# Order of the first U blocks, the bias rows, and the split of two Wq blocks in a one-core decoder layer

## The chip, the cores and the metric

The kernel runs as one program on one core of a Trainium2 chip. The metric is the device time of one execution in microseconds (us). The time shown is the median of three executions; one further execution was recorded with a profile, and all rows below are from that one. Times in the rows count from the first instruction of the profiled span.

## The reference

One decoder layer over 512 tokens of width 1024, in float32 (cut to what matters here):

```python
a = rmsnorm(h, attn_norm)
proj = a @ w_in                       # q, k, v of both head groups
# differential attention, 4 heads, two maps each, T5 relative bias on both maps
bias = rel_bias[t5_bucket(max(dist, 0))]            # (query, key) -> head
logits = q @ k * scale + bias;  softmax;  attn = probs[0] - lam * probs[1]
# retention, 4 heads; then h += concat(A, B) @ w_out
m = rmsnorm(h, ffn_norm)
scores = (m @ w_query) . sub_keys     # 8 heads x 2 x 128 keys, top 16 of each
expert, gates = the 16 best of the 16 x 16 sums per head, softmax
h += sum over selected e of gate_e * gelu(m . u[e]) * v[e]   # 16384 experts
h += sigmoid(rmsnorm(h) @ Wg + bg) * (p @ Wp)
out = rmsnorm(h, final_norm)
```

## The kernel before, in words

Products of float32 operands are made from two parts of each operand, a rounded high part (`wh`, `xh`) and the rest (`wl`, `xl`), with three products each (`product3`, matmul line 85). Each weight block of 128 x 1024 (512 KB) is loaded by SyncE (SP), its high part is copied by ScalarE (ACT) and its low part is made by a subtraction on VectorE (DVE). In `prepare` there is a second way for the low part: ACT writes the negated high part (line 758), and a DMA on GpSimd's (POOL's) queue adds the raw block to it in place (line 759).

**First stage (attention input).** Token products for one group of values, then the projection blocks in the order of the list `blocks`. `project_tile` multiplies one block and cuts the next one (`ahead`, ACT line 179 and DVE line 185). After the first projection tile come the token scales `rr`/`rT` (lines 132 and 291) and then the bias rows. The T5 bias of a head is a function of the distance alone, so one row of 640 values holds it. `relw` repeats the bias table of each head 128 times, and a product with the one-hot table `bucket` (in two pieces, 512 and 128 columns) gives the row on all 128 partitions; ACT copies the two pieces to `bias_s` (line 341) and POOL's queue stores it in DRAM as `bias_d[h]` (line 342). This is done for four heads in a row. The product tile `pb` has two buffers, which it shares with `rr`. `table(h)` (line 378) later reads `bias_d[h]` back from the same POOL queue with a row step of 639, which gives the Toeplitz table `toep` that the scores of the head add (line 388). POOL also makes copies of half of each q block (line 302) between these DMAs.

**Wq stage.** Sixteen blocks of the expert query matrix, called units ("q", c). Units 0 and 1 are loaded and split while the output projection still runs, with the low part on DVE. Units 2 to 15 use the way over POOL's accumulating DMA. In each step c of the loop at line 965 the kernel issues loads, prepares unit c+2, multiplies unit c, copies the result on ACT (line 981), multiplies the result of step c-1 with its sub-keys (`score`, line 952) and ranks the scores of step c-2 on DVE.

**U stage.** The expert matrix U has 128 blocks. 384 of the tokens meet all experts with a dense product and gate weights that are zero outside the selection; the other 128 tokens fetch their selected rows with indirect DMAs (`gather`, `sparse_step`). The loop at line 1185 multiplies block n, and lets VectorE build the gate weights beside it from a generator (`steps`). The work is placed by hand-written clocks in microseconds (`clock["pe"]`, `["dve"]`, `["dma"]`): a generator step is drawn while the DVE clock is behind the PE clock, and a gathered row or a write of gate weights is placed when the DMA clock lets it. Blocks 0 to 23 (`KEEP`) stay on chip in `kept`; `finish` puts the Gelu of their products there (line 793), and the part of the tokens whose gate weights are already known is multiplied with them by `weigh` (line 799). When the gate weights of 8 tokens come, `tail` multiplies the kept blocks that are done (line 1133, DVE) and copies the weights for those that are not (line 1130, ACT). Blocks from 24 on go out to DRAM: Gelu into `av` (line 809) and a store of 192 KB on SP's queue (`spill`, line 817), one iteration later. After 96 iterations a second loop goes through the V blocks and the rest of U (line 781), and the gate and the final norm end the program.

Of the kernel before, what the change touches and what calls it, by code (L numbers as in the profile page):

```python
# [23 lines left out]
F32 = mybir.dt.float32  # L24
# [11 lines left out]
P = 128  # L36
# [18 lines left out]
def block_kernel(ctx: ExitStack, tc, t):  # L55
# [89 lines left out]
    with pool("wa", 2, side="right") as wa, pool("sm", 2, side="right") as sm, \  # L145
# [67 lines left out]
        with pool("proj", side="right") as pj, pool("att", 2, side="right") as at:  # L213
# [69 lines left out]
                    nc.scalar.activation(val[which, b], ps[b], AF.Copy, scale=ra[:, b:b + 1])  # L283

            first_q = project_tile()
            relw = at.tile([33, 4, P], F32, name="relw", tag="rp")
            nc.vector.tensor_copy(relw, relx[:, :, None].to_broadcast([33, 4, P]))
            rr = psM.tile([P, S], F32, name="rr", tag="misc")
            token_rows(at.tile([P, 4, P], F32, name="dg", tag="rx", bufs=3), rr, ra)
            rT = pj.tile([P, S], F32, name="rT")  # L290
# [42 lines left out]
                dqk[a, m, z] = yield from (stack_q, stack_k)[z](m, x)  # L333


            for h in range(4):
                bias_s = at.tile([P, 640], F32, name="bias_s", tag="pr", bufs=3)
                for x, c0, c1 in bucket:
                    pb = psM.tile([P, 512], F32, name="pb", tag="misc")
                    nc.tensor.matmul(pb[:, :c1 - c0], relw[:, h], x, start=True, stop=True)  # L340
                    nc.scalar.activation(bias_s[:, c0:c1], pb[:, :c1 - c0], AF.Copy)
                nc.gpsimd.dma_start(bias_d[h], bias_s)

            for m, z in ((0, 1), (1, 0), (1, 1)):
                ps = project_tile()
# [389 lines left out]
        def prepare(u, low):  # L735
            kind, i = u
            w = raw.pop(u)
            if kind == "g":
                for d in range(2):
                    c = slice(d * S, (d + 1) * S)  # L740
                    scaled_split(fin["gh"][i][d], fin["gl"][:, i, c], w[:, c], gains[:, G_PLE, i:i + 1])
                return
            wh = wt.tile([P, D], F32R, name="wh", tag="wh")
            wl = wt.tile([P, D], F32R, name="wl", tag="wl")
            nc.scalar.activation(wh, w, AF.Copy)  # L745
            parts[u] = wh, wl
            if kind == "v":
                gv, av = inputs.pop(u)
                if gv is not None:
                    av3 = av.rearrange("p (z t) -> p z t", t=RUN)  # L750
                    nc.vector.tensor_tensor(av3, gv, av3, op=OP.mult)
                ah = vp[0].tile([P, ND], F32R, name="ah", tag="ah", bufs=2)
                al = vp[0].tile([P, ND], F32R, name="al", tag="al", bufs=2)
                nc.scalar.activation(ah, av, AF.Copy)  # L754
                parts[u] += ah, al
            if low is nc.gpsimd:

                nc.scalar.activation(wl, w, AF.Copy, scale=-1.0)
                nc.gpsimd.dma_start(wl.bitcast(F32), w, accum_op=OP.add)
            else:  # L760
                low.tensor_tensor(wl, w, wh.bitcast(F32), op=OP.subtract)  # L761
            if kind == "v":
                nc.vector.tensor_tensor(al, av, ah.bitcast(F32), op=OP.subtract)  # L763

        def products(u):
            kind, i = u
            if kind in "uq":
                n = ND if kind == "u" else S
                wh, wl = (x.rearrange("p (k e) -> p k e", k=KC) for x in parts.pop(u))
                ps = mm.tile([P, S], F32, name="ps", tag="mm")  # L770
                project(ps[:, :n], (wh, wl), mx, slice(0, n))
                made[u] = ps
            elif kind == "v":
                vh, vl, wh, wl = parts.pop(u)
                first, last = count[0] == 0, count[0] == P - 1
                count[0] += 1
                for b in range(NT):
                    c = slice(b * P, (b + 1) * P)
                    for a, bb, f, l in ((wh, vh, first, False), (wh, vl, False, False), (wl, vh, False, last)):
                        for d in range(2):  # L780
                            nc.tensor.matmul(acc[b][d], a[:, c], bb[:, d * S:(d + 1) * S], start=f, stop=l)  # L781
# [140 lines left out]
    with pool("pk") as pk, pool("psG", 2, space=PSUM) as psG, pool("psT", space=PSUM) as psT:  # L922
# [3 lines left out]
        def top16(lists):  # L926
# [8 lines left out]
            for v, ix, src, tmp in lists:  # L935
                nc.vector.max_index(ix[:, 8:16], v[:, 8:16], tmp)

        iof = pk.tile([P, P], F32, name="iof", tag="tmp", bufs=2)
        nc.sync.dma_start(iof, t["iota"])
        io2 = pk.tile([P, P, 2], BF16, name="io2")  # L940
# [1 line left out]
        nc.sync.dma_start(prf[:, :3 * TOPK], t["pairs"])  # L942
        pairs = pk.tile([P, 3, TOPK, TOPK], BF16, name="pairs")
        with pool("qs", 2) as qs:
            units = [("q", c) for c in range(16)] + [("u", n) for n in range(RAW - 1)]
            loaded, prepared = 2, 2
            sks, qt, scores = {}, {}, {}

            def score(c):
                sc = psT.tile([P, 4, P], F32, name="sc", tag="sc")  # L950
                for b in range(4):
                    nc.tensor.matmul(sc[:, b], qt[c][:, b * P:(b + 1) * P], sks[c], start=b == 0, stop=b == 3,  # L952
                                     skip_group_check=True)
                scores[c] = qs.tile([P, 4, P], F32, name="scs", tag="scs", bufs=3)
                nc.scalar.activation(scores[c], sc, AF.Copy)

            def rank(c):
                ic = qs.tile([P, 4, TOPK], U32, name="ic", tag="ic")
                for b in (0, 2):
                    top16([(vals[:, z, c], ic[:, z], scores[c][:, z],  # L960
                            pk.tile([P, P], F32, name="tmp", tag="tmp", bufs=2)) for z in (b, b + 1)])
                nc.vector.tensor_copy(idx[:, :, c], ic)

            for c in range(16):
                while loaded < min(len(units), c + RAW):
                    load(units[loaded])
                    loaded += 1
                while len(sks) < min(16, c + RAW):
                    k = len(sks)
                    sks[k] = qs.tile([P, P], F32, name="sk", tag="sk", bufs=RAW + 1)  # L970
                    nc.sync.dma_start(sks[k], t["sk_t"][k])
                while prepared < min(len(units), c + 3):
                    prepare(units[prepared], nc.gpsimd if units[prepared][0] == "q" else nc.vector)
                    prepared += 1
                if c == 0:
                    nc.vector.tensor_copy(io2, iof[:, :, None].to_broadcast([P, P, 2]))
                    nc.vector.tensor_copy(pairs.rearrange("p z a k -> p (z a) k"),
                                          prf[:, :3 * TOPK, None].to_broadcast([P, 3 * TOPK, TOPK]))
                products(("q", c))
                qt[c] = qs.tile([P, S], F32, name="q", tag="q")  # L980
                nc.scalar.activation(qt[c], made.pop(("q", c)), AF.Copy)
                if c:
                    score(c - 1)
                if c > 1:
                    rank(c - 2)
            score(15)
            rank(14)
            rank(15)
# [195 lines left out]
        n = 0  # L1184
        while busy or later or after or n % QUAD:
            unit[0] = n
            load(("u", n + RAW - 1))
            prepare(("u", n + 2), nc.vector)
            clock["dve"] += 1.25
            for f in after:  # L1190
                clock["dve"] += f()
            after.clear()
            gather()
            spill(0)
            finish(("u", n - 1) if n else None, False)
            clock["pe"] += 4.1
            clock["dma"] = max(clock["dma"], clock["pe"] - BACK) + LOAD + (PART if n > KEEP else 0.0)
            free = [x for x in later if not (writes and writes[0][2] <= x[3] - 2) and n >= x[4]][:2]
            later[:] = [x for x in later if x not in free]
            products(("u", n))  # L1200
            for c, f, a, g, _ in free:
                f(*a)
                clock["pe"] += c
            if soon:
                nc.scalar.activation(*soon.pop(0), AF.Copy)

            for g in {x[3] for x in later if x[1].__name__ == "tail"} | {x[3] for x in free if x[1].__name__ == "tail"}:
                made_at[g] = n
            while (writes and n >= made_at[writes[0][2]] + 2 and clock["dma"] + LOAD <= clock["pe"] + SLACK):
                f, q, g = writes.pop(0)  # L1210
                f(*q)
                clock["dma"] += 1.1 * LOAD
            while clock["dve"] < clock["pe"]:
                c = next(steps, None)
                if c is None:
                    busy = False
                if c is None or c == WAIT:
                    clock["dve"] = max(clock["dve"], clock["pe"] - 5.0)
                    break
                clock["dve"] += SLOW * c  # L1220
            n += 1
# [286 lines left out]
```

## Time and profile before

| | |
|---|---|
| time, median of 3 | 1568.82 us (1565.44 to 1569.31) |
| the profiled execution's own time | 1566.29 us |
| its span | 1564.5 us |
| TensorE (PE) busy | 1525.8 us, 98% |
| VectorE (DVE) busy | 1220.9 us, 78% |
| ScalarE (ACT) busy | 680.2 us, 43% |
| GpSimd (POOL) busy | 384.2 us, 25% |
| mean granted clock of TensorE | 0.991 |

Busy shares are averages over stages with different limits. A busy PE may still run at the lower granted clock, or issue small products.

### The profile page before, as it was taken

The page shows a single profiled execution, that of the slowest core. Times are in us where ns is not written, and L with a number is a line of the kernel's source. Part 1 is how long each engine was busy: PE and PEld are TensorE (multiplying, and loading weights), DVE is VectorE, ACT ScalarE, POOL GpSimd, SP SyncE. Part 2 cuts the span into 40 slices and gives each one's busy share as a digit, 9 for nine tenths or more (in the row PEclk, how much of TensorE's full clock was granted, in tenths as well). Part 3 has the DMA queues.
Part 4 walks back from the last instruction along what each step waited for, and adds up shares of the span by engine and source line. Part 5 has one row for each costly group of instructions (what it writes and reads, how often), then busy time and mean ns, then how long its engine had stood idle before and what let it go on. Part 6 is the DMA issues. An engine that isn't in the chain of part 4 may idle for free.

```text
span 1564.5 us, 22940 instructions
## 1 busy us (share of the span) xinstructions
PE 1525.8 (98%) x8209; PEld 1346.2 (86%) x8209; DVE 1220.9 (78%) x2523; ACT 680.2 (43%) x1077; POOL 384.2 (25%) x311
## 2 busy tenths in 40 slices
PE   8999999899999999999999999999999999999996
PEld 6687888688989999999999889898989898888885
DVE  3577665478998998898995889989888875797755
ACT  5455554444644454344443333333333333353444
POOL 1200000110012203211323556554434210522000
PEclk9899999999999999999999999999999999999999
DMA  6322335775358987987999999999999988899601
GB/s 236 101 81 68 115 101 202 192 177 146 123 174 273 290 277 263 317 289 244 311 324 344 375 340 375 332 383 390 369 341 380 348 326 319 310 404 349 244 23 41
DMA packets 163474, 402.72 MB, mean 257 GB/s; under 512 B 14527, under 2 KB 77258, under 8 KB 163232
## 3 DMA queue, kind: packets, MB, share of 16 engines
q1 hardware_dynamic: 123248, 256.06, 46.3%
q0 software_dynamic: 40112, 145.20, 27.5%
q8 instruction: 64, 1.05, 0.3%
q14 instruction: 50, 0.41, 0.1%
HBM read 350.61 MB, written 42.21 MB: 251 GB/s over the span
## 4 chain that ended last, share of the span: by engine, by line
PE 88%; DVE 5%; DMA 3%; ACT 2%; issue 1%; SPq 0%; POOL 0%; ACTq 0%; DVEq 0%; POOLq 0%
PE ps L85 42%; PE acc L781 33%; PE S L85 3%; PE S L322 1%; PE ps L517 1%; PE pg L1118 1%; PE pg L1120 1%; PE wo L85 1%; DVE wl L761 1%; PE sc L952 1%; PE po L457 1%; DMA wraw<-in_w_val_dram 1%; PE po L638 1%; DMA row<-in_peer_v_dram,e_sp 1%; DMA row<-in_peer_u_dram,e_sp 1%
## 5 line engine op out<-in xcount | busy, mean ns | idle before, releaser
L85 PE MATMUL ps<-xh,wh 128*128 128x384 f32 (+1 forms) x1312 | 464.6, 354 | 3.6 <-ACT av L809 2.7
L85 PE MATMUL ps<-xh,wl 128*128 128x384 f32 (+1 forms) x1312 | 458.1, 349 | 8.8 <-DMA wl<-wraw 4.5
L85 PE MATMUL ps<-xl,wh 128*128 128x384 f32 (+1 forms) x1320 | 458.1, 347 | 0.0
L745 ACT ACTIVATE wh<-wraw 128x1024 fp32r<-128x1024 f32 x272 | 286.8, 1054 | 196.1 <-PE ps L85 105.1
L761 DVE TENSOR_TENSOR wl<-wraw,wh 128x1024 fp32r<-128x1024 f32 x258 | 314.5, 1220 | 70.4 <-ACT wh L745 66.0
L847 POOL DMA_INDIRECT row<-in_peer_u_dram,e_sp x128 | 174.9, 1366 | 392.1 <-DVE yacc L860 241.9
L85 PEld LDWEIGHTS ps<-xh,wl 128*128 128x128 f32 x1312 | 247.7, 189 | 22.6 <-DVE wl L761 5.8
L85 PEld LDWEIGHTS ps<-xh,wh 128*128 128x128 f32 x1312 | 248.3, 189 | 16.8 <-ACT av L809 3.6
L85 PEld LDWEIGHTS ps<-xl,wh 128*128 128x128 f32 x1320 | 249.5, 189 | 10.6
L847 POOL DMA_INDIRECT row<-in_peer_v_dram,e_sp x128 | 173.0, 1351 | 341.2 <-DVE act L858 255.8
L781 PE MATMUL acc<-wh,ah 128*128 128x512 f32 x768 | 236.7, 389 | 0.8 <-ACT ah L754 0.8
L781 PE MATMUL acc<-wl,ah 128*128 128x512 f32 x768 | 236.6, 389 | 0.0
L781 PE MATMUL acc<-wh,al 128*128 128x512 f32 x768 | 236.6, 389 | 0.0
L781 PEld LDWEIGHTS acc<-wh,al 128*128 128x128 f32 x768 | 144.1, 188 | 30.2 <-DVE al L763 0.2
L781 PEld LDWEIGHTS acc<-wh,ah 128*128 128x128 f32 x768 | 143.9, 188 | 30.5 <-ACT ah L754 1.2
L781 PEld LDWEIGHTS acc<-wl,ah 128*128 128x128 f32 x768 | 144.1, 188 | 30.2 <-DVE wl L761 0.2
L860 DVE SCALAR_TENSOR_TENSOR yacc<-row,act,yacc 128x1024 f32<-128x1024 f32 x128 | 163.6, 1278 | 5.1 <-DMA row<-in_peer_v_dram,e_sp 5.0
L858 DVE CUSTOM_DVE_ANT_0 junk<-row,mtok 128x1024 bf16<-128x1024 f32 x128 | 155.8, 1217 | 2.4 <-DMA row<-in_peer_u_dram,e_sp 2.1
L754 ACT ACTIVATE ah<-av 128x384 fp32r<-128x384 f32 x104 | 54.6, 525 | 230.0 <-PE acc L781 184.4
L763 DVE TENSOR_TENSOR al<-av,ah 128x384 fp32r<-128x384 f32 x104 | 57.7, 554 | 65.0 <-ACT ah L754 64.9
L1128 ACT ACTIVATE gs<-pg 128x832 f32<-128x832 f32 x48 | 41.5, 866 | 146.4 <-PE pg L1120 122.1
L185 DVE TENSOR_TENSOR wl<-wraw,wh 128x1024 fp32r<-128x1024 f32 x33 | 40.6, 1230 | 28.4 <-ACT wh L179 28.2
(288 smaller groups left out, 1710.7 us busy)
## 6 DMA issues: line engine op xcount, KB each, us to landing
wraw<-in_u_t_dram SPq DMA_DIRECT2D x128, 512.0 KB
wraw<-in_peer_v_dram SPq DMA_DIRECT2D x128, 512.0 KB
gv<-g_d SPq DMA_DIRECT2D x26, 768.0 KB
g_d<-gs SPq DMA_DIRECT2D x24, 576.0 KB
a<-av SPq DMA_DIRECT2D x72, 192.0 KB
av<-a SPq DMA_DIRECT2D x72, 192.0 KB
wraw<-in_w_in_t_dram SPq DMA_DIRECT2D x16, 512.0 KB
wraw<-in_wq_t_dram SPq DMA_DIRECT2D x16, 512.0 KB
```

Source lines behind the costliest of these rows:

```text
L85: nc.tensor.matmul(out, a, b, start=first and k == 0, stop=last and k == n - 1)
L185: nc.vector.tensor_tensor(cut_w[k][1], raw_w.pop(k), cut_w[k][0].bitcast(F32), op=OP.subtract)
L322: nc.tensor.matmul(out, *((a, b) if q_first else (b, a)), start=n == 0, stop=n == 1)
L745: nc.scalar.activation(wh, w, AF.Copy)
L754: nc.scalar.activation(ah, av, AF.Copy)
L761: low.tensor_tensor(wl, w, wh.bitcast(F32), op=OP.subtract)
L763: nc.vector.tensor_tensor(al, av, ah.bitcast(F32), op=OP.subtract)
L781: nc.tensor.matmul(acc[b][d], a[:, c], bb[:, d * S:(d + 1) * S], start=f, stop=l)
L847: nc.gpsimd.indirect_dma_start(out=rows[n], out_offset=None, in_=t[table], in_offset=bass.IndirectOffsetOnAxis(ap=e_sp[:, r:r + 1], axis=0))
L858: nc.vector.tensor_tensor_reduce(junk, row, mtok, 1.0, 0.0, OP.mult, OP.add, act[:, r:r + 1])
L860: nc.vector.scalar_tensor_tensor(yacc, row, act[:, r:r + 1], yacc, op0=OP.mult, op1=OP.add)
L1128: nc.scalar.activation(gs[0][:, :, t0:t0 + 8], pgi[:, KEEP:], AF.Copy, scale=2.0 ** -15)
```

## The change

Three edits. The bias rows of all four heads come from one product per piece: `relw` repeats each head's table 32 times, so that 32 partitions belong to each head, and the store to `bias_d` is made in 16 DMAs of 32 partitions in place of 4 of 128. Units 2 and 3 of Wq take their low part from DVE, as units 0 and 1 do. In the U stage the order of the first 28 blocks is 24, 25, 26, 27, 0, 1, ..., 23 in place of 0 to 27; the names of the blocks that are kept stay the same.

```diff
             first_q = project_tile()
-            relw = at.tile([33, 4, P], F32, name="relw", tag="rp")
-            nc.vector.tensor_copy(relw, relx[:, :, None].to_broadcast([33, 4, P]))
+            relw = at.tile([33, 4, 32], F32, name="relw", tag="rp")
+            nc.vector.tensor_copy(relw, relx[:, :, None].to_broadcast([33, 4, 32]))
...
+            bias_s = at.tile([P, 640], F32, name="bias_s", tag="pr", bufs=3)
+            for x, c0, c1 in bucket:
+                pb = psM.tile([P, 512], F32, name="pb", tag="misc")
+                nc.tensor.matmul(pb[:, :c1 - c0], relw.rearrange("p h r -> p (h r)"), x, start=True, stop=True)
+                nc.scalar.activation(bias_s[:, c0:c1], pb[:, :c1 - c0], AF.Copy)
             for h in range(4):
-                bias_s = at.tile([P, 640], F32, name="bias_s", tag="pr", bufs=3)
-                for x, c0, c1 in bucket:
-                    pb = psM.tile([P, 512], F32, name="pb", tag="misc")
-                    nc.tensor.matmul(pb[:, :c1 - c0], relw[:, h], x, start=True, stop=True)
-                    nc.scalar.activation(bias_s[:, c0:c1], pb[:, :c1 - c0], AF.Copy)
-                nc.gpsimd.dma_start(bias_d[h], bias_s)
+                for q in range(4):
+                    nc.gpsimd.dma_start(bias_d[h, 32 * q:32 * q + 32], bias_s[32 * h:32 * h + 32])
...
+        def early(n):
+
+            return "u", KEEP + n if n < QUAD else n - QUAD if n < KEEP + QUAD else n
...
-            units = [("q", c) for c in range(16)] + [("u", n) for n in range(RAW - 1)]
+            units = [("q", c) for c in range(16)] + [early(n) for n in range(RAW - 1)]
...
-                    prepare(units[prepared], nc.gpsimd if units[prepared][0] == "q" else nc.vector)
+                    prepare(units[prepared], nc.gpsimd if units[prepared][0] == "q" and prepared > 3 else nc.vector)
...
-            load(("u", n + RAW - 1))
-            prepare(("u", n + 2), nc.vector)
+            load(early(n + RAW - 1))
+            prepare(early(n + 2), nc.vector)
...
-            finish(("u", n - 1) if n else None, False)
+            finish(early(n - 1) if n else None, False)
             clock["pe"] += 4.1
-            clock["dma"] = max(clock["dma"], clock["pe"] - BACK) + LOAD + (PART if n > KEEP else 0.0)
+            clock["dma"] = max(clock["dma"], clock["pe"] - BACK) + LOAD + (PART if early(n)[1] >= KEEP else 0.0)
...
-            products(("u", n))
+            products(early(n))
```

## Rows read from the trace of the kernel before

**Rows 1.** Busy time by stretch; columns: stretch, its length, engines, PEclk, DMA share, GB/s.

```profile
core 0: us, PE busy (x) PEld busy (x) DVE busy (x) ACT busy (x) POOL busy (x), PEclk, DMA share, GB/s
38.00:49.00 11.00, 8.27 (x18) 4.14 (x18) 0.00 (x0) 5.79 (x14) 1.63 (x3) 0.70 0.25 97
285.00:302.00 17.00, 11.64 (x50) 9.13 (x49) 4.97 (x33) 7.84 (x10) 2.66 (x3) 0.80 0.87 223
386.00:449.00 63.00, 56.76 (x323) 54.97 (x321) 62.13 (x275) 33.84 (x41) 3.04 (x3) 1.00 0.38 123
449.00:1490.00 1041.00, 1037.55 (x5777) 940.86 (x5776) 881.20 (x1330) 420.37 (x601) 344.82 (x253) 1.00 0.91 324
```

**Rows 2.** Timeline 30 to 62 us: start, duration, engine, line, count [idle before, releaser].

```profile
37.95 1.34 PE L340 MATMUL pb<-bucket,relw 33*128 33x512 f32 x4
...
40.83 0.79 ACT L341 ACTIVATE bias_s<-pb 128x512 f32<-128x512 f32 x2
...
41.91 0.55 POOL L342 DMA_DIRECT2D bias_d<-bias_s  x1 [36.10 <-ACT bias_s L341]
...
48.62 0.79 PE L85 MATMUL ps<-xh,wh 128*128 128x512 f32 x1
...
50.04 1.23 DVE L185 TENSOR_TENSOR wl<-wraw,wh 128x1024 fp32r<-128x1024 f32 x1 [13.37 <-ACT wh L179]
...
52.63 0.39 PE L85 MATMUL ps<-xh,wh 128*128 128x512 f32 x1
...
52.86 0.40 PE L85 MATMUL ps<-xl,wh 128*128 128x512 f32 x1
```

**Rows 3.** Timeline of POOL, 0 to 80 us.

```profile
3.66 0.56 POOL L231 DMA_DIRECT2D lam<-in_lam_k_dram  x1
4.19 0.56 POOL L231 DMA_DIRECT2D lam<-in_lam_q_dram  x1
...
63.13 2.15 POOL L302 CAST q<-q 64x512 fp32r<-64x512 f32 x2 [8.38 <-ACT q L301]
65.23 0.54 POOL L378 DMA_DIRECT2D toep<-bias_d  x1
```

**Rows 4.** Timeline 59 to 90 us: the first scores and the first use of the table.

```profile
72.40 0.22 PE L322 MATMUL S<-k,q 128*128 128x128 f32 x1
...
73.42 0.29 DVE L388 CUSTOM_DVE_ANT_0 pr<-S,toep 128x128 f32<-128x128 f32 x1
```

**Rows 5.** Chain of work that ended last, 270 to 420 us: start, duration, what.

```profile
280.02 5.09 DMA wraw<-in_wq_t_dram
...
287.45 6.35 DMA wl<-wraw
```

**Rows 6.** Timeline of ACT, 275 to 312 us.

```profile
285.14 1.06 ACT L745 ACTIVATE wh<-wraw 128x1024 fp32r<-128x1024 f32 x1 [7.55 <-DMA wraw<-in_wq_t_dram]
...
287.05 0.58 ACT L981 ACTIVATE q<-ps 128x512 f32<-128x512 f32 x1
287.53 1.04 ACT L745 ACTIVATE wh<-wraw 128x1024 fp32r<-128x1024 f32 x1
```

**Rows 7.** Timeline of PE, 275 to 330 us.

```profile
286.48 0.39 PE L85 MATMUL ps<-xh,wl 128*128 128x512 f32 x1
287.68 1.16 PE L952 MATMUL sc<-sk,q 128*128 128x128 f32 x8 [0.82 <-ACT q L981]
...
301.08 1.06 PE L952 MATMUL sc<-sk,q 128*128 128x128 f32 x8
...
307.45 1.06 PE L952 MATMUL sc<-sk,q 128*128 128x128 f32 x8
```

**Rows 8.** The page's costliest groups: count, then busy and mean ns.

```profile
L761 DVE TENSOR_TENSOR wl<-wraw,wh 128x1024 fp32r<-128x1024 f32 x258 | 314.5, 1220 | 70.4 <-ACT wh L745 66.0
```

**Rows 9.** Timeline of POOL, 225 to 400 us: the accumulating DMAs.

```profile
292.67 0.86 POOL L759 DMA_DIRECT2D wl<-wraw  x1 [1.98 <-DMA wl<-wraw]
...
304.96 0.86 POOL L759 DMA_DIRECT2D wl<-wraw  x1 [11.42 <-ACT wl L758]
```

**Rows 10.** Waits of SP's queue, whole span: total us, times, longest.

```profile
SPq L817 <- ACT av L809: 204.3, 58, 8.7
```

**Rows 11.** Instructions of lines 1133 and 796: ns min/median/max, first and last start.

```profile
L1133 DVE SCALAR_TENSOR_TENSOR kept<-pg,kept x48: 267/350/352, 463.0 to 831.8; 128x192 f32<-128x192 f32 x41, 128x184 f32<-128x184 f32 x2, 128x112 f32<-128x112 f32 x1, 128x128 f32<-128x128 f32 x1
...
L796 ACT ACTIVATE av<-ps x10: 167/194/253, 462.0 to 505.3; 128x8 f32<-128x8 f32 x2, 128x16 f32<-128x16 f32 x2, 128x32 f32<-128x32 f32 x2, 128x40 f32<-128x40 f32 x2
```

## The prediction

> **What bounds the kernel now.** I read the busy table by stretch first. From 449 to 1490 us TensorE (PE) is busy 1037.55 of 1041 us at full clock, so that nothing beside PE can be worth much there: all waits of PE in two thirds of the span are 3.5 us [rows 1]. The same table shows two holes in front of it. From 38 to 49 PE is busy 8.27 of 11 us at a mean clock of 0.70, and from 285 to 302 it is busy 11.64 of 17 us at 0.80; two of the three edits sit exactly there [rows 1]. The third sits in 386 to 449, where VectorE (DVE) is busy 62.13 of 63 us and PE waits for it, and in the first blocks after 449 [rows 1]. Then I read the timeline around both holes for what ends each wait, and the chain of waits around 280 us. Between the holes, from 49 to 285 us, the chain runs over products and over ACT and DVE work fed by them, not over loads. So time won in the first hole should move all that follows it.
>
> **Edit 1, the bias rows.** Before, the product of the first head takes from 37.95 to 39.29 us, and the other three heads alternate with ACT's copies until the next projection block starts at 48.62 [rows 2]. Its low part was cut a block ahead; the subtraction at 50.04 is already for the block after it [rows 2]. With one group of products the projection can start at 39.3, 9.3 us earlier. It also started slowly: from 48.62 to 52.63 nine products of 512 columns took 4.01 us, that is the lower of the two clock levels (1.2 GHz) after the pauses for ACT, where the next one takes 0.23 us at 2.4 GHz (52.63 to 52.86) [rows 2]. Nine at the full level are 2.07 us, so 1.9 us more come back, since PE now pauses for half a microsecond only. Together 11.3 us.
>
> What this costs is on POOL's queue: 16 issues where there were 4. The two copies of ACT start at 40.83 and the first store could go at 41.91 as before [rows 2]. Small DMAs in a row on that queue stand 0.53 us apart (3.66 to 4.19), and a bias store takes 0.55 [rows 2, 3]. So 16 of them at 0.54 end at 41.91 + 8.6 = 50.6. Behind them wait the copies of q, two pairs of 2.15 us (54.9), and the read of the table, 0.54 (55.4) [rows 3]. How long that read takes no row shows; a load of 512 KB took 5.09 [rows 5], the table has 256 KB, so by 60.5 it is there. The first use was at 73.42, the first scores at 72.40 [rows 4]; shifted by 11.3 they come at 62.1 and 61.1. The cover is 1.6 us at least for the table and 6 for the copies, so I cost the 16 issues at nothing. If each took 0.86 us, as the accumulating DMA does [rows 9], the table would come at 65.7 and 3.6 us would be lost: this edit gives 7.7 to 11.3.
>
> The Trainium skill (DMA: Bandwidth & Descriptors, "Anatomy of one DMA") speaks against this edit: each DMA of POOL's queue costs about 2.0 us plus bytes over 436 GB/s whatever its size. An estimate from that page, were the costs paid one after the other, is 16 x 2.19 = 35.0 us, with the table at 86.8 and 24.7 us late, which turns the sum below into a loss of 5.6. The page puts most of the 2 us into completion, not into the issue, and the 0.53 us between issues here agree with that reading.
>
> **Edit 2, units 2 and 3 of Wq.** The raw block of unit 2 lands at 285.11 (280.02 + 5.09), and the accumulating DMA for its low part takes 6.35 us from 287.45, to 293.80 [rows 5]. PE has by then scored unit 0 and stands; the next score comes at 301.08, and a full step is 6.37 us (301.08 to 307.45) [rows 7]. After the change: ACT makes the high part from 285.14 to 286.20, and goes to the copy of q, 0.58 us, without the negated copy between, so it is done at 286.8 and not at 287.6 [rows 6]. The score of unit 0, which waited 0.82 for that copy [rows 7], starts when the product of unit 1 ends, at 286.86. DVE's subtraction takes 1.22 us [rows 8], to 287.4; the product of unit 2 wants it at about 287.8. The next score comes at 286.86 + 6.37 = 293.23, which is 7.85 us earlier. Unit 3: ACT took its raw block at 287.53 without waiting for the load [rows 6], so its low part is there by 287.53 + 1.04 + 1.22 = 289.8, and two short conversions of DVE fit before; it is needed at 294.1. Unit 4 is the first over the accumulating DMA. Even issued as late as before, at 292.67 [rows 9], it lands at 299.0 and is needed at 300.5; with less in front of it, it should be issued some 2 us earlier. DVE has nothing else to do up to the first ranking. If unit 4 came late by the 5 us that it would cost to land after a full second transfer, 2.9 would be left: 2.9 to 7.9, and I take 7.8.
>
> **Edit 3, the order of the first blocks.** The four stores of 192 KB move from the iterations 26 to 29 to 2 to 5. There SP's loads stand behind them, and each waits for a Gelu. Before, 58 such waits held SP for 204.3 us, 3.5 us each [rows 10], and PE lost at most 3.5 us in all of that stretch [rows 1], so four are worth 0.2 us or less; the memory is at 0.38 in the early stretch against 0.91 later [rows 1]. Below, nothing; above, if each reached PE, 4 x 3.5 = 14 us.
>
> On DVE and ACT I followed the planner's clocks through the loop. With the old order the first nine `tail` calls meet 14, 16, 18, 19, 21, 23, 23, 24, 24 finished blocks, with the new one 10, 12, 14, 15, 17, 19, 19, 21, 23: 32 fewer in sum, 8 columns each. Line 1133 costs (350 - 267) / (192 - 112) = 1.04 ns a column (the 112 is the first call, 14 x 8) [rows 11], so DVE saves 0.3 us. Four more blocks end after weights are known, each with one more short Gelu of 0.19 us [rows 11] and one short multiplication. The planner's DMA clock misses three additions of 0.55 at iterations 25 to 27, by which 65 gathered rows in place of 64 are worked off in this loop; the loop still has 96 iterations, and the three turns of the weights come at 12, 41 and 69 as before. All of it is beside a PE that is full. What PE loses in 386 to 449 hangs on DVE's choice of experts, which the order does not touch. I cost this edit at nothing.
>
> **The sum.** 11.3 + 7.8 = 19.1 us off the profiled execution's 1566.29 (span 1564.5, 1.8 around it) is 1547.2. That execution is 2.5 us under the median of 1568.82; off the median the sum gives 1549.7. I forecast between the two, 1548.5.
>
> **The rivals.**
> (a) Both holes close but part is given back: the POOL issues are as slow as 0.86 us, unit 4 is late, or a DVE already full in 386 to 449 is reached no earlier. The last has against it that DVE's work there starts from ACT and PE results of the Wq stage. One of the two terms alone gives 1557 to 1561, losses of 3 to 5 us give 1552 to 1554.
> (b) Slower than before: POOL's queue holds back issues until earlier DMAs of its own have landed. For it: at 292.67, with two accumulating DMAs issued, POOL waited 1.98 us for one of them [rows 9]. Were that the rule, two stores at 0.86 and fourteen at 0.86 + 1.98 = 2.84 end at 83.4; with 4.30 of copies, 0.54 and 5.09 the table comes at 93.3, 31.2 late, and the sum turns into 12 us lost: about 1580. The point from which it decides is 1.83 us per store (41.91 + 16 x 1.83 + 9.93 = 62.1 + 19.1). Against it: the issues at 0.53 us in a row without a wait, and the stores are 80 KB where the accumulating DMA moves 512 [rows 3, 9].
> (c) More than the sum: with the early stores out of the loaded stretch and 0.3 us less for DVE, PE's 3.5 us of waits after 449 go, or the one full stop before 449 gets shorter because ACT and DVE arrive in another order: 1540 to 1545.
> (d) The order costs: one gathered row more before iteration 41, 1.2 us of DVE, makes PE wait for a turn, or the four stores hold SP's loads in a stage that has no slack: 2 to 14 us, 1551 to 1562.
>
> **How the numbers follow.** The forecast, both terms whole within 2 to 3 us, has 0.70 and gives 1544 to 1552. (a) and (d) together have 0.18, (c) 0.07, (b) 0.03, and 0.02 that neither hole closes as read (the time stays). A measurement tells changes of 0.3%, 4.7 us, from none. All of the forecast and of (c), and nearly all of (a) and (d), are faster than that: 0.94; 0.03 within, 0.03 slower. The range of 1541 to 1557 leaves out the single-term cases, (b) and the far end of (c).
>
> **What would show it.** Right: the product line 85 starts at 39 to 40 us and runs at 0.23 us from there; line 340 has 4 PE instructions and not 16; the first scores stand at 61; the second score of Wq comes 6.4 us after the first; PE's clock is 1.00 in both stretches; the wait of PE for the accumulating DMA is gone; units after 449 look as before, 19 us earlier. Wrong: DVE's line 388 waits for the table, POOL's issues of line 342 are more than 1 us apart, a wait for the accumulating DMA appears at unit 4, or PE's waits in the U stage grow beyond a few microseconds.

## The result, and the profile after

The changed kernel takes 1545.61 us (median of 4, 1544.91 to 1546.94) against 1568.09 us for the kernel before (median of 4, 1565.44 to 1569.31). The ratio is 0.986, with a 95% interval of 0.9843 to 0.9877: faster. The forecast was 1548.5 us, so the time came out 2.9 us lower, inside the range of 1541 to 1557 and inside the 1544 to 1552 that the forecast was given. The profiled execution took 1544.91 us with a span of 1543.1 us, 21.4 us less than the span before.

The busy table by stretch of the changed kernel, with the columns of [rows 1]. The first two stretches lie where the holes stood; the third and the fourth hold the work that [rows 1] has from 386 to 449 and from 449 to 1490:

```profile
38.00:49.00 11.00, 11.00 (x49) 8.65 (x49) 4.92 (x6) 6.83 (x11) 5.91 (x12) 1.00 0.55 165
270.00:290.00 20.00, 19.98 (x100) 16.68 (x100) 12.88 (x70) 9.16 (x12) 1.79 (x2) 1.00 0.88 253
367.50:430.50 63.00, 57.60 (x323) 56.52 (x322) 62.13 (x275) 33.85 (x41) 3.06 (x3) 0.97 0.40 135
430.50:1468.50 1038.00, 1036.69 (x5776) 941.26 (x5775) 881.83 (x1334) 420.88 (x607) 340.52 (x253) 1.00 0.91 324
```

Both holes of [rows 1] are closed: PE is busy 11.00 of 11 us and 19.98 of 20 us, at full clock. The third line is the stage that DVE sets, and there PE still stands. The fourth line is the one that the prediction did not have: PE's gaps in the long stretch were 3.5 us in 1041 and are 1.3 us in 1038.

The timeline of the changed kernel around the first hole (start, duration, engine, line [idle before, releaser]), against [rows 2 to 4]:

```profile
38.37 1.34 PE L339 MATMUL pb<-bucket,relw 33*128 33x512 f32 x4
39.64 0.51 PE L85 MATMUL ps<-xh,wh 128*128 128x512 f32 x1
39.98 0.40 PE L85 MATMUL ps<-xl,wh 128*128 128x512 f32 x1
40.22 0.40 PE L85 MATMUL ps<-xh,wl 128*128 128x512 f32 x1
...
41.25 0.79 ACT L340 ACTIVATE bias_s<-pb 128x512 f32<-128x512 f32 x2
...
42.33 5.91 POOL L343 DMA_DIRECT2D bias_d<-bias_s  x12 [36.51 <-ACT bias_s L340]
49.57 1.96 POOL L343 DMA_DIRECT2D bias_d<-bias_s  x4 [1.33 <-DMA bias_d<-bias_s]
51.57 2.34 POOL L302 CAST q<-q 64x512 fp32r<-64x512 f32 x2
54.11 2.15 POOL L302 CAST q<-q 64x512 fp32r<-64x512 f32 x2 [0.19 <-ACT q L301]
56.21 0.55 POOL L379 DMA_DIRECT2D toep<-bias_d  x1
...
62.61 0.29 DVE L389 CUSTOM_DVE_ANT_0 pr<-S,toep 128x128 f32<-128x128 f32 x1
```

Four instructions of the bias product stand where there were sixteen, and the projection's products follow 0.24 us apart from 39.98 on, the distance at the higher clock level (1.00 in the table). The stores go out 0.50 us apart. The queue stopped once, after twelve, for 1.33 us. The table is issued at 56.21; its four reads land in 2.8 to 3.8 us (the source view of line 379), so it is there by 60.0 and used at 62.61.

The chain of waits of the changed kernel around the second hole (start, duration, line), and the second score in PE's timeline, against [rows 7]:

```profile
264.90 11.21 PE ps L85 x48
276.14 1.13 PE sc L957 x8
277.27 5.48 PE ps L85 x24
282.75 0.89 PE sc L957 x8
```

```profile
282.59 1.06 PE L957 MATMUL sc<-sk,q 128*128 128x128 f32 x8
```

The second score starts 6.45 us after the first (276.14 to 282.59), and products fill the time between. All of PE's waits from 36 to 300 us are 0.7 us or less each, and none of them is for the accumulating DMA.

PE's waits from the ranking on, first the kernel before (378 to 1565 us), then the changed one (360 to 1543; line waited for: us in total, times, longest):

```profile
PE ps L85 <- DVE wl L761: 4.2, 3, 2.0
PE ps L85 <- ACT av L809: 2.7, 3, 1.8
PE pt L1092 <- DVE ij L1075: 2.0, 1, 2.0
PE acc L781 <- ACT ah L754: 0.8, 1, 0.8
PE sc L952 <- ACT scs L955: 0.7, 1, 0.7
```

```profile
PE ps L85 <- DVE wl L762: 3.4, 2, 2.1
PE pt L1097 <- DVE ij L1080: 1.9, 1, 1.9
PE ps L85 <- ACT av L810: 0.8, 1, 0.8
PE sc L957 <- ACT scs L960: 0.7, 1, 0.7
PE acc L782 <- ACT ah L755: 0.6, 1, 0.6
```

The wait for the Gelu `av` went from 2.7 to 0.8 us. The longest of the three, 1.8 us, stands in the kernel before between the V blocks 88 and 92, some 900 us after the blocks whose order was changed. The 0.8 us for `ah` stand there too. To see where each microsecond was won I took the start of the same piece of work in each trace:

```
start, us before each marker of the kernel before (positive: earlier)
                   before    after     e1      e2      e3      e4      e9
first Wq score      287.7     11.6    11.0     0.7    -2.4    10.9     9.8
U block 0           386.5     18.5    11.2     7.7    -2.7    17.9    16.9
U block 14          454.6     18.5    11.1     7.7    -2.7    19.4    21.3
first V block       862.0     19.0    10.9     8.6    -2.5    20.0    21.8
V block 88         1321.3     19.0    10.9     8.6    -2.5    20.0    21.8
V block 92         1357.3     22.0    12.1     9.0     0.5    18.1    24.8
end of span        1564.5     21.4    10.7     8.9     0.2    18.3    25.0
```

Up to V block 88 the changed kernel is 19.0 us ahead, the predicted sum of 19.1. Then 3.0 us come within four blocks. The table compares one execution with one: the first bias product itself starts at 37.95 us in the kernel before, at 38.37 in the changed one, and between 37.7 and 40.2 in the traces of all the runs below. The experiments ask which edit these gains belong to, and by what means. Experiments of one set ran on one chip with the same runs of the kernel before: e1 to e4 against 1567.39 us (17 runs), e5 to e8 against 1568.51 (11), e9 and e10 against 1567.46 (9), e11 and e12 against 1567.64 (9). One execution of e8, of 6867.53 us at a mean granted clock of 0.208, was in a slow state and is left out of e8's median.

### The profile page after: what moved, and what is told of

The parts are those of the page before. It is cut to its first block, busy times and chain, and to the rows that moved or that the text cites. A ratio compares the mean times of both kernels' runs of the same rounds, so it can differ in the third digit from the quotient of the medians.

```text
span 1543.1 us, 22928 instructions
## 1 busy us (share of the span) xinstructions
PE 1515.5 (98%) x8197; PEld 1342.0 (87%) x8197; DVE 1223.0 (79%) x2529; ACT 676.4 (44%) x1075; POOL 384.1 (25%) x321
## 4 chain that ended last, share of the span: by engine, by line
PE 88%; DVE 7%; DMA 3%; ACT 1%; issue 1%; SPq 0%; ACTq 0%; DVEq 0%
PE ps L85 44%; PE acc L782 31%; PE S L85 2%; PE S L322 2%; PE ps L518 1%; PE pg L1123 1%; PE pg L1125 1%; PE wo L85 1%; DVE wl L762 1%; PE sc L957 1%; DMA wraw<-in_w_val_dram 1%; DMA av<-a 1%; PE po L458 1%; PE po L639 1%; DMA wraw<-in_gate_w_dram 1%
## 5 line engine op out<-in xcount | busy, mean ns | idle before, releaser
L762 DVE TENSOR_TENSOR wl<-wraw,wh 128x1024 fp32r<-128x1024 f32 x260 | 317.4, 1221 | 77.5 <-ACT wh L746 76.8
L848 POOL DMA_INDIRECT row<-in_peer_v_dram,e_sp x128 | 169.6, 1325 | 374.2 <-DVE act L859 277.3
L752 DVE TENSOR_TENSOR av<-gv,av 128x384 f32<-128x384 f32 x104 | 57.5, 553 | 7.4 <-DMA av<-a 6.8
```

The source lines that it names most:

```text
L848: nc.gpsimd.indirect_dma_start(out=rows[n], out_offset=None, in_=t[table], in_offset=bass.IndirectOffsetOnAxis(ap=e_sp[:, r:r + 1], axis=0))
```

## The experiments: the edits one by one

**e1: the bias rows alone.** The edits of `relw`, of the product and of the 16 stores, on the kernel before.

> The bias rows by one product alone; Wq and the order of U as before. My theory: the three edits act in stages that lie one behind the other, so their gains add, and this one gives the shift that the changed kernel shows in front of the Wq stage, 10.8 us (products of unit 0 at 275.69 before, 264.90 after), carried whole to the end: 0.9931 of before. Rival: stages further on run by loads, and part of it is waited away there: 0.995 to 0.998. In the trace I expect POOL to wait once between the stores after twelve of them, as in the changed kernel, with no one waiting for POOL.

Measured: 1555.07 us (6), ratio 0.992 [0.9905, 0.9934]. The shift is 11.0 to 11.2 us over the whole Wq stage, and PE is busy 11.00 us from 38 to 49. Counted within one trace, from the first bias product to the first scores, it is the same: 34.45 us in the kernel before, 23.18 here. The second hole is still there: PE's only wait of over 0.7 us between 36 and 300 us is this one.

```profile
PE ps L85 <- DMA wl<-wraw: 3.5, 1, 3.5
```

**e2: the two Wq blocks alone.**

```diff
-                    prepare(units[prepared], nc.gpsimd if units[prepared][0] == "q" else nc.vector)
+                    prepare(units[prepared], nc.gpsimd if units[prepared][0] == "q" and prepared > 3 else nc.vector)
```

> Units 2 and 3 of Wq split by VectorE alone. My theory: 7.5 us, the difference of the shifts in front of and behind the first steps of that stage (10.8 and 18.3), carried to the end: 0.9952 of before. Rival: a unit further on comes late over the accumulating DMA, because PE reaches it sooner, and 3 us are left: 0.998.

Measured: 1557.62 us (6), ratio 0.9942 [0.9929, 0.9956]. The shift at U block 0, right behind the last score, is 7.7 us, and the first two scores are 6.37 us apart (286.99 and 293.36), exactly a full step of [rows 7]. Here the first hole is the only long wait left (`bias_s`, 2.9 us).

**e3: the order alone.** `early` and its five uses, on the kernel before.

> The order of the first U blocks alone; bias rows and Wq as before. My theory, as predicted: nothing, within 0.3% of before, since PE is full after 449 us. Rival: the medians fell by 22.5 us where the two holes give 18 to 19, and the order gives the rest, 2.3 to 3.5 us (0.9978 to 0.9985), by PE waits in the V stage between 1325 and 1360 us that are gone.

Measured: 1564.84 us (12), ratio 0.9981 [0.9973, 0.999]: 0.19%, or 3.0 us, and the interval lies clear of 1. In the profiled execution the first scores come 2.5 us later than in that of the kernel before (74.88 and 72.40), which the table above carries through as -2.5: the first bias product starts 1.4 us later, and from it to the scores it takes 1.1 us longer. At V block 88 nothing has been won; four blocks later 3.0 us have. So the late gain belongs to the order, and it needs neither of the other edits.

**e4: the bias rows and the Wq blocks, with the old order.**

> The bias rows and Wq without the order of U. My theory: the two gains add to 18.3 to 19 us, 0.988 of before, some 3 us above the changed kernel, if the order is worth what the medians leave over. Rival: it equals the changed kernel (0.986), and what the sum lacked lies in the shift itself, for example where gathered rows and loads meet in the V stage.

Measured: 1548.45 us (4), ratio 0.9879 [0.9865, 0.9893]. That is the forecast of 1548.5 us, whose sum has both terms whole and nothing from the order. To the tenth it is luck: e4's trace is 20.0 us ahead at V block 88, where the sum has 19.1, and falls 1.9 us back on the four blocks after it. The V blocks 88 to 92 take 37.9 us here, against 33.0 in the changed kernel.

## The experiments: the order or the count of rows

The edit of the order does two things. It moves four blocks and their stores, and through the planner's DMA clock (`PART`) it lets 65 gathered rows in place of 64 be worked off in the first loop. The prediction noted the second and set it aside.

**e5: the new order, with 64 rows.** On the changed kernel:

```diff
-            clock["dma"] = max(clock["dma"], clock["pe"] - BACK) + LOAD + (PART if early(n)[1] >= KEEP else 0.0)
+            clock["dma"] = max(clock["dma"], clock["pe"] - BACK) + LOAD + (PART if n > KEEP else 0.0)
```

> The changed kernel, but the planner's DMA clock takes its PART at the iterations of before (n > KEEP), so that with the new order 64 gathered rows, and not 65, are worked off in the U loop. Theory R (the row count makes the order's 2.5 to 3 us): DVE's wait of 4 to 5 us for a gathered row near the end of the V stage comes back with PE's stop behind it, V block 88 to 92 takes 35 to 38 us in place of 33.0, and the time is that of bias rows and Wq without the order, 1548 to 1549. Theory O (where the stores stand makes it): as the changed kernel, 1545.6.

Measured: 1548.67 us (4), ratio 0.9879 [0.9862, 0.9897], as e4. The V blocks 88 to 92 take 37.5 us.

**e6: the old order, with 65 rows.** On e4:

```diff
-            clock["dma"] = max(clock["dma"], clock["pe"] - BACK) + LOAD + (PART if n > KEEP else 0.0)
+            clock["dma"] = max(clock["dma"], clock["pe"] - BACK) + LOAD + (PART if n > KEEP + 3 else 0.0)
```

> Bias rows and Wq as changed, the order of U as before, but the planner's DMA clock takes its PART only from iteration 28 on (n > KEEP + 3), so that 65 rows are worked off in the U loop with the old order. Theory R: PE's stop near the end of the V stage is gone, V block 88 to 92 takes 33.0 us, and the time is that of the changed kernel, 1545 to 1546. Theory O: as without the order, 1548.5.

Measured: 1544.27 us (4), ratio 0.9855 [0.9838, 0.9872], as the changed kernel. The V blocks 88 to 92 take 33.0 us. With e4 and the changed kernel this is a square of two by two: 64 rows give 1548.5 and 1548.7 with either order, 65 rows give 1544.3 and 1545.6. The count decides, and the place of the blocks and of their stores makes no difference beyond the intervals. The intervals of the two counts overlap a little (0.9862 to 0.9897 for e5, 0.9838 to 0.9872 for e6); what parts them is the stop at the V blocks 88 to 92, which each trace with 64 rows has and none with 65.

What the row does is in these lines. The busy table over the V blocks 88 to 92, of the kernel before, of e5, and of the changed kernel:

```profile
1321.30:1357.30 36.00, 33.46 (x169) 29.95 (x168) 25.72 (x32) 11.98 (x18) 13.97 (x12) 1.00 0.86 285
```

```profile
1301.50:1339.00 37.50, 34.91 (x170) 31.74 (x169) 26.98 (x34) 12.99 (x18) 15.33 (x12) 0.95 0.86 289
```

```profile
1302.30:1335.30 33.00, 33.00 (x169) 30.19 (x168) 26.24 (x34) 12.99 (x18) 13.81 (x12) 1.00 0.90 322
```

DVE has 7 to 10.5 us to spare in each. What differs is one stop in its queue. DVE's timeline there, of the kernel before and of the changed one:

```profile
1331.82 1.22 DVE L858 CUSTOM_DVE_ANT_0 junk<-row,mtok 128x1024 bf16<-128x1024 f32 x1
...
1337.07 1.28 DVE L860 SCALAR_TENSOR_TENSOR yacc<-row,act,yacc 128x1024 f32<-128x1024 f32 x1 [4.03 <-DMA row<-in_peer_v_dram,e_sp]
...
1338.74 1.22 DVE L761 TENSOR_TENSOR wl<-wraw,wh 128x1024 fp32r<-128x1024 f32 x1
```

```profile
1312.82 1.22 DVE L859 CUSTOM_DVE_ANT_0 junk<-row,mtok 128x1024 bf16<-128x1024 f32 x1
...
1314.39 1.28 DVE L861 SCALAR_TENSOR_TENSOR yacc<-row,act,yacc 128x1024 f32<-128x1024 f32 x1 [0.34 <-DMA row<-in_peer_v_dram,e_sp]
...
1316.07 1.22 DVE L762 TENSOR_TENSOR wl<-wraw,wh 128x1024 fp32r<-128x1024 f32 x1
```

In the kernel before DVE stands 4.03 us for a gathered row, where it is 0.34 us in the changed kernel. How that reaches PE, in the timeline of the kernel before:

```profile
1338.27 0.55 DVE L751 TENSOR_TENSOR av<-gv,av 128x384 f32<-128x384 f32 x1
1338.86 0.52 ACT L754 ACTIVATE ah<-av 128x384 fp32r<-128x384 f32 x1 [4.06 <-DVE av L751]
1339.29 0.47 ACT L809 ACTIVATE av<-ps 128x384 f32<-128x384 f32 x1
1339.81 0.44 PE L85 MATMUL ps<-xh,wh 128*128 128x384 f32 x1 [1.77 <-ACT av L809]
```

Behind the row in DVE's queue stands the multiplication for the next V block (line 751). ACT's copy of its result (754) waits 4.06 us for it, the Gelu that reads PE's product `ps` (809) stands behind that copy in ACT's queue, and PE waits for the Gelu. In e1, e2, e4, e5 and e8 PE's stop there ends with the same Gelu, after 1.5 to 3.0 us. The subtraction for the next weight block (line 761) stands behind the row too, 6.9 us after the row step before it (line 858) where it is 3.3 in the changed kernel. It ends at 1339.96, and the first product that reads it starts at 1340.27: without the wait for the Gelu, PE would have stood for the subtraction about as long (an estimate from these starts).

In e5 the stop is 4.84 us, in e6 there is none. The gather of that row on POOL and its use on DVE, first in e5, then in e6:

```profile
1309.53 1.74 POOL L848 DMA_INDIRECT row<-in_peer_v_dram,e_sp  x1 [3.04 <-DVE act L859]
1318.12 1.28 DVE L861 SCALAR_TENSOR_TENSOR yacc<-row,act,yacc 128x1024 f32<-128x1024 f32 x1 [4.84 <-DMA row<-in_peer_v_dram,e_sp]
```

```profile
1305.53 0.94 POOL L848 DMA_INDIRECT row<-in_peer_v_dram,e_sp  x1 [0.60 <-DVE act L859]
1313.22 1.28 DVE L861 SCALAR_TENSOR_TENSOR yacc<-row,act,yacc 128x1024 f32<-128x1024 f32 x1
```

DVE was ready for the row at 1313.28 in e5 and at 1313.22 in e6, but the gather was issued 4.0 us later in e5; in both it was issued when a row buffer that DVE had read came free. The fourteen traces line up on this:

```
V blocks 88 to 92: rows worked off in the first loop, longest wait of DVE
for a gathered row (us), time of the four blocks (us)
64 rows:  before 4.03, 36.0   e1 3.76, 34.8   e2 4.03, 35.6
          e4 5.28, 37.9       e5 4.84, 37.5
65 rows:  after 1.14, 33.0    e3 1.15, 33.0   e6 0.88, 33.0   e7 1.34, 33.3
          e9 0.82, 33.0       e11 1.11, 33.0  e12 0.98, 33.0
66 rows:  e10 1.67, 33.0
67 rows:  e8 4.58, 35.6
```

A wait of 1.7 us costs nothing, one of 3.8 to 5.3 us costs 1.8 to 4.9 us. Part of this price is the clock: in e4 and e5 PE's stop of 3.0 and 2.6 us was followed by 3.4 us at a granted clock of 0.50, and the products of the four blocks took 34.9 us in place of 33.0 (0.95 in the table of e5). In the kernel before and in e1, e2 and e8 the clock stayed at 1.00 there.

**e10: the old order, with 66 rows.** Is more better, or is it which row falls where? On e4, with `n > KEEP + 4` in the line of e6.

> Bias rows and Wq as changed, the old order of U, and the PART of the DMA clock taken only from iteration 29 on, so that 66 rows are worked off in the U loop. Theory A (the stop at the end of the V stage is a matter of which row falls where, and 65 is a lucky count): the stop is back in some size, V block 88 to 92 takes 34 to 38 us, 1546 to 1549. Theory B (the more rows early, the less is left for the end): no stop, 33 us, 1544 to 1545.

Measured: 1545.76 us (4), ratio 0.9859 [0.9842, 0.9876]. The stop at V block 88 is away, and the time is not under that of e6. So the second row more gives nothing, and e8 below, with 67, has the stop again. It is not that more rows are better; which row meets which block is what the timelines leave. That the three row buffers left in this stretch set the moment at which a gather is issued is argued from the issue times above; no run changes the buffers.

## The experiments: the price of the stores, and a later turn

**e7: 32 stores in place of 16.** The same bytes for the rows kept, but each of 16 partitions (on the changed kernel; each half store reads the first 16 partitions of its group, which hold the same values):

```diff
-                for q in range(4):
-                    nc.gpsimd.dma_start(bias_d[h, 32 * q:32 * q + 32], bias_s[32 * h:32 * h + 32])
+                for q in range(8):
+                    nc.gpsimd.dma_start(bias_d[h, 16 * q:16 * q + 16], bias_s[32 * h:32 * h + 16])
```

> The changed kernel with the bias rows stored in 32 DMAs of 16 partitions in place of 16 of 32 (the same rows, other copies of them). Theory (POOL's cost is its issue of 0.50 us, with a wait of 1.3 us after each dozen): POOL ends the stores some 9 to 10 us later, at 60 to 61 us, the copies of q at 65, the table lands at 69; the first scores, at 62 in the changed kernel, come 4 to 7 us late, 1550 to 1553. Rival (a fixed 2 us for each DMA of that queue, one after the other): 32 us more, 1570 or above. Rival (something else covers it): no change.

Measured: 1547.53 us (4), ratio 0.9869 [0.9851, 0.9888], 0.9 thousandths over the changed kernel and within its interval. POOL's timeline of this run, and DVE's first use of the table:

```profile
43.29 5.77 POOL L343 DMA_DIRECT2D bias_d<-bias_s  x12 [37.46 <-ACT bias_s L340]
49.35 8.14 POOL L343 DMA_DIRECT2D bias_d<-bias_s  x17 [0.29 <-DMA bias_d<-bias_s]
57.87 1.44 POOL L343 DMA_DIRECT2D bias_d<-bias_s  x3 [0.38 <-DMA bias_d<-bias_s]
59.35 2.97 POOL L302 CAST q<-q 64x512 fp32r<-64x512 f32 x4
62.27 0.56 POOL L379 DMA_DIRECT2D toep<-bias_d  x1
...
65.34 0.29 DVE L389 CUSTOM_DVE_ANT_0 pr<-S,toep 128x128 f32<-128x128 f32 x1 [0.61 <-DMA toep<-bias_d]
```

The table is issued 6 us later, of which 1 us is a later start of the first bias product in this execution (39.33 and 38.37). The cover that edit 1 leaned on is now used up: DVE waits 0.61 us for the table, which it does neither in the kernel before nor in the changed one. The loss that I expected was too large: the stores ended at 59.3 us and not at 60 to 61, the four copies of q took 2.97 us in all in place of 4.69, and the table was there 3.1 us after its issue (62.27 to 65.34), where the expectation has 4 from the end of the copies. The copies had a price of their own: the small DVE operations beside them (line 355) took 0.52 and 0.63 us, 0.23 each in the changed kernel, and PE waited 0.63 us for the subtraction that came after (line 185).

**e8: the turn of the weights one iteration later.** In the stage that DVE sets, PE's waits are for `wl` and for the `ij` that is turned on PE. On the changed kernel, a first value of the planner's DVE clock that draws the steps later:

```diff
-        clock = {"pe": 0.0, "dve": 3, "dma": 0.0}
+        clock = {"pe": 0.0, "dve": 5, "dma": 0.0}
```

> The changed kernel with the planner's DVE clock started at 5 in place of 3, by which the first turn of the weights comes one U block later (iteration 13, not 12) and 67 rows are worked off in the U loop. Theory: PE's waits between 368 and 431 us (two for low parts from DVE, 3.4 us in all, and 1.9 at the turn) are there because DVE has more to do before the turn than 12 blocks cover; a 13th block covers it, and 2 to 4 us are won: 1542 to 1544. Rival: what is won at the turn comes back at the end of the V stage, since the row count has changed: 1545 to 1548.

Measured: 1544.35 us (5), ratio 0.9848 [0.9834, 0.9862]. From U block 0 to U block 14 it takes 63.6 us, the changed kernel 68.1: 4.5 us won. At the V blocks 88 to 92 it loses 2.6 us, since the later steps also let 67 rows be worked off.

**e9: the later turn, with 65 rows.** e8 with the edit of e5.

> The changed kernel with the DVE clock started at 5, as in the run with the later turn, and the PART of the DMA clock taken at n > KEEP, so that 65 rows and not 67 are worked off in the U loop. Theory: the two effects add. U block 14 starts some 3 us sooner than in the changed kernel, as in the run with the later turn, and V block 88 to 92 takes 33 us again: 1541 to 1542.5. Rival: the end of the V stage hangs on more than the row count, its stop is there, and the time stays at 1544.

Measured: 1541.59 us (5, 1539.3 to 1542.93), ratio 0.9834 [0.9818, 0.985]. Both gains are there: 63.6 us to U block 14 and 33.0 us at the V blocks 88 to 92. The busy table from just before U block 0 to just before U block 14, of the changed kernel and of e9, shows what the 4.5 us are:

```profile
367.50:436.00 68.50, 63.10 (x346) 62.02 (x346) 66.91 (x281) 36.10 (x47) 3.06 (x3) 0.95 0.39 135
```

```profile
369.00:433.00 64.00, 61.14 (x345) 60.52 (x344) 63.08 (x275) 35.41 (x43) 3.46 (x3) 0.97 0.42 139
```

PE stands 2.9 us in place of 5.4, and its nearly equal number of products takes 2.0 us less, at a higher mean clock. By the waits, that for `ij` fell from 1.9 to 0.9 us and that for `wl` from 3.4 to 2.0. The clock's part is not sure to be there each time. The changed kernel was granted 0.50 from 378.9 to 382.3 and from 430.1 to 433.5, e9 only from 380.8 to 384.2. But e4, e7 and e10, with the turn and the three stops of the changed kernel (2.0, 1.4 and 2.0 us), kept 1.00 through the stage (370 to 440 us), and took 66.6 us from U block 0 to 14. So of the 4.5 us some 3 are the stops, and 1.5 hang on the clock.

**e11 and e12: the changed kernel and e9 again, side by side.**

> The changed kernel once more, on the same chip as the next one. Theory: 0.986 of before again, 33 us from V block 88 to 92, and PE's waits before the first turn (5 us) as they were.

> The kernel with the later turn and 65 rows once more, beside the changed kernel. Theory: 4 us below the changed kernel, 0.983 of before, since its 13th block covers what DVE has to do before the turn and the end of the V stage stays free of the stop. Rival: the 4 us between chips were chance, and the two agree within 1.5 us.

Measured: e11 1545.98 us (4), ratio 0.9854 [0.9834, 0.9873]; e12 1541.12 us (5, 1540.15 to 1541.97), ratio 0.9827 [0.981, 0.9843]. No time of e9 or e12 reaches the fastest of either set of the changed kernel (1543.72), so this version beats both kernels, by 26.5 us the one before and by 4.9 us the changed one.

## Why the prediction was right, and where its sum fell short

**Edit 1, 11.3 us, held.** e1 shows 11.0 to 11.2 us of shift, and 11.3 counted from the first bias product to the first scores. The pieces held too: the projection starts 1.27 us after the first bias product (predicted 1.35), at the full clock. On POOL the stores took 0.50 us and not 0.54, but one pause of 1.33 us put their end at 51.5 where 50.6 was predicted; the table landed by 60.0 (predicted 60.5) for a use at 62.61 (predicted 62.1). Rival (b) had its mechanism in that pause, but once in 16 stores, far from the 1.83 us per store from which it would have decided. The series of 2.19 us per DMA that was estimated from the Trainium skill (DMA: Bandwidth & Descriptors, "Anatomy of one DMA") did not come: 16 issues took 9.2 us with the pause. That page's reading that most of the fixed cost is completion agrees with the landing times here, 2.0 to 5.0 us for a store whose issue took 0.50.

**Edit 2, 7.8 us, held.** e2 shows 7.7 us and a step of 6.37 us; in the changed kernel the step is 6.45. Unit 4 was not late: no wait for an accumulating DMA is left, so 2.9 us, the lower bound, did not come into play. Nothing in the DVE stage behind took this back for good (rival (a)). There was one sign of it: at U block 3 the lead had fallen from 18.5 to 17.0 us, after a stretch at the lower clock, and by block 12 it was 18.5 again, since DVE, and not PE, sets the end of that stage.

**Edit 3, at nothing, is the term that was mis-sized: it gave 3 us.** The step that failed is the sentence that 65 rows in place of 64, beside everything else in the loop, are "beside a PE that is full". The count of rows was right, the price was wrong. It was read from sums over 1041 us, in which 3.5 us of waits look like nothing, without asking at which place they stood. Two stops within four V blocks, 1.8 and 0.8 us, were 2.5 of these 3.5 us; the 169 products there took 0.5 us more (33.46 and 33.00 us), and these are the 3.0. e5 and e6 show that the count of rows does this, with either order. Rival (c) named the size (1540 to 1545) and the waits that would go, but its reasons, the stores out of the loaded stretch and DVE's 0.3 us, are not what did it: e5 has both and loses the gain. The column saving itself came as worked out: the first call of line 1138 is now one of 80 columns, ten blocks. The stores' waits on SP grew from 204.3 [rows 10] to 217.6 us, and PE lost nothing by them, so rival (d) did not show.

The single edits give 0.992 x 0.9942 x 0.9981 = 0.9844, just inside the interval of 0.986. Taken by their medians e1 and e2 alone win 2 to 3 us more than e4; the stop at the V blocks 88 to 92 is large enough for that (those blocks are shorter than before in e1 and e2, by 1.2 and 0.4 us, and longer by 1.9 in e4), read from one profile each.

**What stays open.** Why a given count of rows meets the stop is argued from issue times and not shown by a run that changes the buffers alone. Why the same stops of PE were followed by a stretch at the lower clock level in some executions and not in others, no run shows. That e10's profiled execution ends 3.1 us behind that of the changed kernel, which its median does not show, lies mostly ahead of the first bias product, which starts at 40.16 us and not at 38.37, after a mean granted clock of 0.66 from 15 to 20 us; 0.5 us more are lost up to the first Wq score and 0.9 us behind V block 92.

## What to carry to other kernels

A hole in front of a full engine is worth its whole length at the end if every stage behind it starts from that engine's results: both holes here came through more than 1000 us, within 1 us (e1 is 11.2 us ahead at U block 0 and 10.9 at V block 88, e2 7.7 and 8.6). A wait of a few microseconds in a long full stretch is one event at one place; find it and ask what moves it, before an edit that shifts the alignment of queues is costed at nothing. To see whether an order or a side effect of it won the time, make the two by two: the new order with the old count, and the old order with the new count.

## What the runs showed of the hardware

POOL's queue took small DMAs 0.48 to 0.50 us apart, but stood until an earlier one had landed: 1.33 us after 12 stores of 80 KB in the changed kernel, 0.30 us after 11 and 1.01 us after 12 in e4; with 40 KB each 0.29 us after 12 stores and 0.38 us after 29 (e7). A store's issue says little of its landing, 2.0 to 5.0 us here. In the stage that DVE sets, stops of PE of about 2 us were followed by 3.4 us at a granted clock of 0.50 in the changed kernel (378.9 and 430.1 us), and the same stops by none in e4, e7 and e10. In e9, where 2.5 us of stops were gone and one of the two slow stretches with them, 4.5 us were won.
